# Merging the groups of full-f32 products in an indexer, a sparse attention and a stick-breaking attention

## The chip, the cores and the metric

The kernel runs on one core of a Trainium2 chip. The metric is the device time of one execution in microseconds. The engines of the core are named as in the profile: PE (TensorE matmuls), PEld (its weight loads), DVE (VectorE), ACT (ScalarE), POOL (GpSimd) and SP (SyncE, which here only issues transfers).

## The reference

Two layers (DEPTH = 2) on 256 tokens of width 2048. Each layer normalises its input, projects it once (`proj = h @ w_in`, 18064 columns) and feeds three token mixers; each mixer's output is gated, projected to 2048, and the three are merged with sigmoid gates before an output projection and the residual add. Cut to what the change touches:

```python
# A: sparse attention. 16 indexer heads score the keys, the best top_k = 64 of each query stay
rel   = einsum('bthd,bsd->bhts', qi, ki)
score = where(causal, einsum('bhts,bth->bts', relu(rel), wi), NEG_INF)
_, idx = top_k(score, 64)
p = softmax(where(valid, q @ ks * dh**-0.5, NEG_INF))     # 8 query heads, 2 key/value heads
o = p @ vs
# C: stick-breaking attention, 8 heads, strictly causal
z = q @ k * dh**-0.5
log_beta, log_keep = log_sigmoid(z), where(strict, log_sigmoid(-z), 0)
after = reverse_cumsum(log_keep) - log_keep
o = where(strict, exp(log_beta + after), 0) @ v
```

The queries and keys of A and of its indexer are rotated (rotary embedding) after the projection. All inputs and the output are float32.

## The kernel before, in words

**Units.** The work is a long row of projections. Each goes in units of 512 KB of weights: SP loads a unit (`raw`, four buffers), ACT rounds it to fp32r (`wh`, L223), DVE subtracts to get the rest (`wl`, L227); `wh` and `wl` have three buffers each. PE multiplies: in the usual unit (`chunk_N`) 8 products of 512 columns with `wh` and 4 with `wl`, all on L237. A chunk of 512 output columns over the 2048 inputs has 8 such units.

**Background steps.** What is not a projection is written as Python generators, the stages. After each unit, `background(mm)` first steps the pending transposes that are due and then advances at most one of the first two stages that are due; a stage's `yield n` means "not before n units from now". PE instructions of a step are put behind the last product of that unit (`issue_after`). Chunks that are wanted feature by feature (`chunk_F`) go through memory to be turned: DVE transposes 32x32 blocks (L265), POOL writes `z` to DRAM in four transfers (L268), two units later POOL reads it back as `zy` in one (L274), and after more units the consumer runs. For the query chunks QA the consumer is `rope_F`: two copies on ACT (L386, L387), and one unit later two products and a sum on DVE (L391, L392, L393), which write four heads of `qaT`. These consumer steps are issued with high priority behind the newest weight conversions (`behind`).

**Order.** An engine works in the order in which its instructions are written. That order is made when the kernel is built: a planner simulates the engines with its own costs, and at each moment gives a free engine the instruction of highest priority that its simulation holds to be ready. Conversions and transposes are marked high; all else goes by its place in the program. If on the chip an input comes later than the planner thought, the engine waits at that instruction.

**The steps that the change touches.** PSUM holds two `acc` tiles for projections and two `mm` tiles (1024 columns each) for everything else; `t4` has four buffers of 1024 columns; `ph`, `pl` one each.

- `index_first` scores tokens 64 to 127 with eight f32 products of 128 columns (L801) in two groups of four, `index` the second half with fp32r products (L830); then DVE selects the 64 best (`choose`, L788 to L791) and writes `bias`.
- `attend(t, c)`, one stage for each half of the queries t and each key/value head c, in the order (0,0), (1,0), (0,1), (1,1). It forms logits (L876 in f32 for t = 0, L873 in fp32r after a split for t = 1), softmax (L880 to L888, the exponentials on ACT at L885), turns the weights through memory, splits them into `ph` and `pl`, and multiplies with the values (L904). The four stages start after the chunk QC of the first four stick-breaking heads; in front of it come the two QA chunks.
- `stick(h0)`, one stage for two heads. It forms scores of two heads with f32 products (L942, L945), takes logarithms on ACT, splits, forms cumulative sums with fp32r products (L964 to L969), exponentials (L971), and the product with the values in f32 (L978, L980). Four stages, two of them in flight.

On the trace one f32 product is recorded as two matmuls.

Of the kernel before, what the change touches and what calls it, by code (L numbers as in the profile page):

```python
# [11 lines left out]
ALU = mybir.AluOpType  # L12
AX = mybir.AxisListType

P = 128
# [33 lines left out]
def trunk(ctx: ExitStack, tc: tile.TileContext, x, w_in, xt, w_a, w_b, w_c, w_out,  # L49
# [66 lines left out]
    def mm_tile():  # L116
        return mp.tile([P, 1024], F32, tag="mm", name=nm("mm"))
# [370 lines left out]
    for layer in range(DEPTH):  # L488
# [304 lines left out]
        def index_first(qi0=qi0, kiT=kiT, wi2=wi2, bias=bias):  # L793

            cb = cst[:, C_CB + P:C_CB + S]
            sc = tp.tile([P, S], F32, tag="sc", bufs=2, name=nm("sc"))[:, :P]
            bs = tp.tile([P, S], F32, tag="bias", bufs=2, name=nm("bias"))
            for g in range(2):
                ps = mm_tile()
                for q in range(4):  # L800
                    nc.tensor.matmul(ps[:, q * P:(q + 1) * P], qi0[:, (g * 4 + q) * P:(g * 4 + q + 1) * P], kiT[:, 0, :P],  # L801
                                     start=True, stop=True)
                rl = t4()[:, :512]
                nc.scalar.activation(rl, ps[:, :512], AF.Relu)
                for q in range(4):
                    i = g * 4 + q
                    if i == 0:
                        nc.vector.tensor_scalar(sc, rl[:, :P], wi2[:, :1], None, op0=ALU.mult)
                    else:
                        nc.vector.scalar_tensor_tensor(sc, rl[:, q * P:(q + 1) * P], wi2[:, i:i + 1], sc,  # L810
                                                       op0=ALU.mult, op1=ALU.add)
# [45 lines left out]
        finish()  # L857
        attended = []

        def attend(t, c, qaT=qaT, kaT=kaT, qk=qk, va=va, bias=bias, attended=attended):  # L860
            n = (t + 1) * P
            ts_ = slice(t * P, (t + 1) * P)
            if t:
                yield 4
                qp = [qk[:, 4 + i * 2:6 + i * 2, :].rearrange("p a (b t) -> p (a b) t", t=P) for i in range(2)]
                with behind():
                    split(*qp, qaT[:, c * 4:c * 4 + 4, ts_])
                yield 2
            ps = mm_tile()
            for q in range(4):  # L870
                if t:
                    for m, (i, j) in enumerate(((0, 0), (0, 1), (1, 0))):
                        nc.tensor.matmul(ps[:, q * n:(q + 1) * n], qp[i][:, q, :], qk[:, j * 2 + c, :],  # L873
                                         start=m == 0, stop=m == 2)
                else:
                    nc.tensor.matmul(ps[:, q * n:(q + 1) * n], qaT[:, c * 4 + q, ts_], kaT[:, c, :n],  # L876
                                     start=True, stop=True)
            lg = t4()
            l3 = lg[:, :4 * n].rearrange("p (h s) -> p h s", h=4)
            nc.vector.scalar_tensor_tensor(l3, ps[:, :4 * n].rearrange("p (h s) -> p h s", h=4), SCALE,  # L880
                                           heads(bias[t][:, :n], 4), op0=ALU.mult, op1=ALU.add)
            mx, sm = small(4), small(4)
            nc.vector.tensor_reduce(mx, l3, op=ALU.max, axis=AX.X, negate=True)  # L883
            for q in range(4):
# [3 lines left out]
            nc.vector.tensor_mul(l3, l3, sm.unsqueeze(2).to_broadcast([P, 4, n]))  # L888
            yield 4
            z = away([l3[:, :, s * P:(s + 1) * P] for s in range(t + 1)], t4()[:, :4 * n])  # L890
            yield 3
            y = lg[:, :4 * n].rearrange("p (u q i) -> p u q i", q=4, i=32)
            back(z, y)
            yield 7
            ph, pl = pair(1024)
            with behind():
                for s in range(t + 1):
                    split(*(v[:, s * 512:(s + 1) * 512].rearrange("p (q a i) -> p q a i", q=4, a=4) for v in (ph, pl)),
                          by_feature(y[:, s * 4:s * 4 + 4]))
            yield 3  # L900
            po = mm_tile()
            for s in range(t + 1):
                for i, (u, v) in enumerate(((va[0], ph), (va[0], pl), (va[1], ph))):
                    nc.tensor.matmul(po[:, :512], u[:, s, c * P:(c + 1) * P], v[:, s * 512:(s + 1) * 512],  # L904
                                     start=s == 0 and i == 0, stop=s == t and i == 2)
            nc.scalar.copy(qaT[:, c * 4:c * 4 + 4, ts_], po[:, :512].rearrange("p (h t) -> p h t", h=4))
            attended.append(c)

        for c in range(2):
            for t in range(NT):  # L910
                start(attend(t, c))
        chunk_F(w, O_QC + 4 * P, hx, KD, partial(use_q, 4))


# [22 lines left out]
                    b[:, 512:768].rearrange("p (h t) -> p h t", h=2))  # L937

        def stick(h0, qcT=qcT, kcT=kcT, vcr=vcr, diag=diag):
            ps = mm_tile()  # L940
            for q in range(2):
                nc.tensor.matmul(ps[:, q * S:(q + 1) * S], kcT[:, h0 + q, 0:P], qcT[:, h0 + q, :],  # L942
                                 start=True, stop=True)
            for q in range(2):
                nc.tensor.matmul(ps[:, 512 + q * P:512 + (q + 1) * P], kcT[:, h0 + q, P:S],  # L945
                                 qcT[:, h0 + q, P:S], start=True, stop=True)
            nk, lb = t4(), t4()
            ab = nc.scalar.activation(nk[:, :768], ps[:, :768], AF.Abs)
            with tc.issue_after(ab.ins):
                nc.scalar.preload_act_table_set("natural_log_exp_and_others")  # L950
            nc.scalar.activation(nk[:, :768], nk[:, :768], AF.Exp, scale=-1.0)
            nc.scalar.activation(nk[:, :768], nk[:, :768], AF.Ln, bias=1.0)
            nc.vector.scalar_tensor_tensor(lb[:, :768], ps[:, :768], 0.0, nk[:, :768],
                                           op0=ALU.min, op1=ALU.subtract)
            nc.vector.scalar_tensor_tensor(nk[:, :768], ps[:, :768], 0.0, nk[:, :768],
                                           op0=ALU.max, op1=ALU.add)
            for d in diag(nk):
                nc.vector.tensor_mul(d, d, smask2)
            pr_ = pair(768)
            split(*pr_, nk[:, :768])  # L960
            yield 8
            pc = mm_tile()
            for i, v in enumerate(pr_):
                nc.tensor.matmul(pc[:, :512], upper_r, v[:, :512], start=i == 0, stop=False)  # L964
            for i, v in enumerate(pr_):
                nc.tensor.matmul(pc[:, :512].rearrange("p (h t) -> p h t", h=2)[:, :, P:S], ones_r,  # L966
                                 v[:, 512:768].rearrange("p (h t) -> p h t", h=2), start=False, stop=i == 1)
            for i, v in enumerate(pr_):
                nc.tensor.matmul(pc[:, 512:768], upper_r, v[:, 512:768], start=i == 0, stop=i == 1)  # L969
            nc.vector.tensor_sub(lb[:, :768], lb[:, :768], pc[:, :768])  # L970
            nc.scalar.activation(lb[:, :768], lb[:, :768], AF.Exp)  # L971
            for d in diag(lb):
                nc.vector.tensor_mul(d, d, smask2)
            yield 5
            po = mm_tile()
            for q in range(2):
                vs_ = slice((h0 + q) * P, (h0 + q + 1) * P)
                nc.tensor.matmul(po[:, q * S:(q + 1) * S], vcr[:, 0, vs_], lb[:, q * S:(q + 1) * S],  # L978
                                 start=True, stop=False)
                nc.tensor.matmul(po[:, q * S + P:(q + 1) * S], vcr[:, 1, vs_],  # L980
                                 lb[:, 512 + q * P:512 + (q + 1) * P], start=False, stop=True)
# [236 lines left out]
```

## Time and profile before

| | |
|---|---|
| median of 3 runs | 2027.87 us (2027.77 to 2027.97) |
| profiled execution, its time | 2027.86 us |
| its span (first to last instruction) | 2026.0 us |
| PE busy | 2017.0 us, 100% of the span |
| DVE / ACT / POOL busy | 1515.5 / 1046.7 / 166.3 us |
| HBM read, written | 415.94 MB, 31.98 MB |
| granted TensorE clock | 0.999 |

The span and 1.86 us around it make up the execution's time. The busy shares are means over the whole program; what counts for a step is who waits for whom at its place. The profile's lines name the kernel line (L237), the tile written and the tiles read, and in brackets the idle time of the engine before the instruction and what ended it.

### The profile page before, as it was taken

What the parts mean: (1) busy time and instruction counts of PE and PEld (TensorE: products, weight loads), DVE (VectorE), ACT (ScalarE), POOL (GpSimd) and SP (SyncE); (2) the same over time, 40 slices, a digit from 0 to 9 for tenths busy, and PEclk for the clock granted to TensorE, in tenths of its full rate; (3) what the DMA queues carried; (4) which work ended last, traced back from release to release, by engine and by line L of the source; (5) the groups of instructions that cost most, each with busy time, mean ns of one, the idle gap of its engine ahead of it and who ended that gap; (6) DMA issues with size and microseconds to landing.
All of it is one profiled execution on the core that took longest, in us unless ns stands there. A gap on an engine that the chain in (4) does not pass through costs nothing.

```text
span 2026.0 us, 25968 instructions
## 1 busy us (share of the span) xinstructions
PE 2017.0 (100%) x9520; PEld 1694.7 (84%) x9520; DVE 1515.5 (75%) x2030; ACT 1046.7 (52%) x1213; POOL 166.3 (8%) x279
## 2 busy tenths in 40 slices
PE   9999999999999999999999999999999999999998
PEld 8889888888888888888888898888888888888887
DVE  8668998888788776555775789988886886756565
ACT  7456545566444454444554564555664444544543
POOL 0110022100010000010100101211000100101000
PEclk9999999999999999999999999999999999999999
DMA  7788678755576577776967876787555766677864
GB/s 260 232 292 240 184 245 280 246 178 166 175 236 195 183 221 234 218 234 213 306 203 232 285 222 200 249 263 246 176 166 177 233 196 193 212 252 214 251 222 151
DMA packets 235008, 449.64 MB, mean 222 GB/s; under 512 B 20992, under 2 KB 38400, under 8 KB 234752
## 3 DMA queue, kind: packets, MB, share of 16 engines
q1 hardware_dynamic: 215248, 389.25, 61.3%
q0 software_dynamic: 17968, 55.59, 8.9%
q10 hardware_dynamic: 1664, 3.15, 0.4%
q8 instruction: 74, 1.21, 0.3%
q14 instruction: 54, 0.44, 0.1%
HBM read 415.94 MB, written 31.98 MB: 221 GB/s over the span
## 4 chain that ended last, share of the span: by engine, by line
PE 100%; DVE 0%; ACT 0%; DVEq 0%; issue 0%
PE acc L237 93%; PE mm L237 3%; PE mm L830 1%; PE mm L904 0%; PE mm L978 0%; PE mm L942 0%; PE mm L873 0%; PE mm L618 0%; PE mm L964 0%; PE mm L876 0%; PE mm L801 0%; PE mm L945 0%; PE mm L980 0%; PE mm L969 0%; PE mm L966 0%; PE mm L995 0%
## 5 line engine op out<-in xcount | busy, mean ns | idle before, releaser
L237 PE MATMUL acc<-wh,s 128*128 128x512 f32 (+2 forms) x5632 | 1381.3, 387 | 0.0
L237 PEld LDWEIGHTS acc<-wh,s 128*128 128x128 f32 x5632 | 1038.8, 188 | 206.0 <-ACT wh L223 0.3
L227 DVE TENSOR_TENSOR wl<-raw,wh 128x1024 fp32r<-128x1024 f32 (+2 forms) x729 | 877.8, 1207 | 424.0 <-ACT wh L223 415.6
L223 ACT CAST wh<-raw 128x1024 fp32r<-128x1024 f32 (+2 forms) x728 | 758.3, 1043 | 837.0 <-PE acc L237 631.5
L237 PE MATMUL acc<-wl,s 128*128 128x512 f32 (+2 forms) x2624 | 691.0, 385 | 0.0
L237 PEld LDWEIGHTS acc<-wl,s 128*128 128x128 f32 x2624 | 487.7, 188 | 99.2
L268 POOL DMA_DIRECT2D z<-zt x184 | 106.9, 587 | 1454.0 <-DVE zt L265 1098.4
L440 DVE SCALAR_TENSOR_TENSOR s<-yT,cst,s 128x256 f32<-128x256 f32 x480 | 212.7, 479 | 0.0
L237 PEld LDWEIGHTS mm<-s,wl 128*128 128x128 f32 x512 | 66.9, 191 | 5.0
L237 PE MATMUL mm<-s,wl 128*128 128x192 f32 x512 | 66.0, 271 | 0.0
L274 POOL DMA_DIRECT2D zy<-z x47 | 33.8, 718 | 246.5 <-DMA z<-zt 127.9
L265 DVE STREAM_TRANSPOSE zt<-acc 128x512 f32<-128x512 f32 x64 | 44.6, 707 | 4.8 <-PE acc L237 4.7
L379 DVE TENSOR_TENSOR s<-zy,s 128x1024 fp32r<-128x1024 f32 x20 | 24.4, 1222 | 17.0 <-ACT s L378 17.0
L378 ACT CAST s<-zy 128x1024 fp32r<-128x1024 f32 x20 | 21.0, 1049 | 26.1 <-DMA zy<-z 18.4
L1070 DVE TENSOR_TENSOR ev<-acc,ev 128x512 f32<-128x512 f32 x32 | 22.0, 688 | 15.5 <-PE acc L237 15.5
L1060 ACT ACTIVATE ev<-acc 128x512 f32<-128x512 f32 x48 | 26.6, 592 | 0.1
L268 POOL DMA_DIRECT2D z<-t x36 | 20.4, 573 | 50.4 <-DVE t L265 49.3
L237 PE MATMUL acc<-s,wh 128*128 128x512 f32 x96 | 24.0, 392 | 0.0
L1071 DVE TENSOR_TENSOR s<-s,ev 128x512 f32<-128x512 f32 x32 | 21.9, 686 | 0.1
L1102 DVE TENSOR_TENSOR t<-acc,t 128x512 f32<-128x512 f32 (+1 forms) x18 | 10.6, 628 | 13.6 <-PE acc L237 13.6
L237 PEld LDWEIGHTS acc<-s,wh 128*128 128x128 f32 x96 | 17.3, 189 | 3.0
L885 ACT ACTIVATE t<-t,sm 128x128 f32<-128x128 f32 (+1 forms) x32 | 14.3, 448 | 9.4 <-DVE sm L883 9.4
(218 smaller groups left out, 867.5 us busy)
## 6 DMA issues: line engine op xcount, KB each, us to landing
raw<-in_w_in_dram SPq DMA_DIRECT2D x555, 512.0 KB, 4.4
raw<-in_w_out_dram SPq DMA_DIRECT2D x64, 512.0 KB, 4.9
zy<-z POOLq DMA_DIRECT2D x47, 512.0 KB, 5.4
z<-zt POOLq DMA_DIRECT2D x184, 128.0 KB, 4.3
raw<-in_w_a_dram SPq DMA_DIRECT2D x32, 512.0 KB, 4.1
raw<-in_w_c_dram SPq DMA_DIRECT2D x32, 512.0 KB, 3.6
raw<-in_w_b_dram SPq DMA_DIRECT2D x32, 512.0 KB, 4.9
raw<-in_w_in_dram SPq DMA_DIRECT2D x16, 256.0 KB, 3.0
```

What stands on the lines that cost most here:

```text
L223: newest_parts[0] = nc.scalar.copy(u[1], u[0])
L227: newest_parts[1] = sub = nc.vector.tensor_sub(u[2], u[0], u[1].bitcast(F32))
L237: newest[0] = nc.tensor.matmul(o, lhsT, rhs, start=start, stop=stop, skip_group_check=True)
L265: nc.vector.transpose(tmp[:, t].rearrange("p b k i -> p k b i"), src.rearrange("p k (b c) -> p k b c", b=4, c=32))
L268: nc.gpsimd.dma_start(z[:, :, :, a, :].rearrange("t b c e -> c (t b) e"), tmp[a * 32:(a + 1) * 32].rearrange("c t b k i -> c (t b) (k i)"))
L274: nc.gpsimd.dma_start(y.rearrange("p (t a) k i -> p t (a k i)", a=4), z.rearrange("t b c a e -> (b c) t (a e)"))
L378: nc.scalar.copy(h, src)
L379: nc.vector.tensor_sub(l, src, h.bitcast(F32))
L440: nc.vector.scalar_tensor_tensor(o, yT[:, c, q:q + S], wq, o, op0=ALU.mult, op1=ALU.add)
L1060: nc.scalar.activation(sg[t], g[t], AF.Sigmoid)
L1070: nc.vector.tensor_mul(sg[t], y[t], sg[t])
L1071: nc.vector.tensor_add(dst, dst, sg[t])
```

## The change

Three parts; the sums and products of the computation stay as they are.

1. `index_first` does its eight f32 products in one group, followed by one activation over 1024 columns, and yields once for 4 units instead of twice for 3.
2. `attend` takes a list of key/value heads. The first half of the queries (t = 0) is done for both heads in one stage: 8 products, one softmax of 1024 columns, one turn through memory, 6 value products in a row. The order of the stages becomes (t = 1, head 0), (t = 0, both heads), (t = 1, head 1). Since the second stage now reads all eight rotated heads, the QA consumer `use_a` notes which four heads it has written (`roped`), and a stage yields unit by unit until its heads are noted.
3. `stick` takes four heads: the scores of both pairs in both `mm` tiles at once, then the element-wise chain of each pair, the cumulative sums pair after pair with 3 units between, and one group of value products for four heads. One stage (`sticks`) runs the two groups of four one after the other; before, four stages of two heads ran two at a time.

The core of the diff:

```diff
-            for g in range(2):
-                ps = mm_tile()
-                for q in range(4):
-                    nc.tensor.matmul(ps[:, q * P:(q + 1) * P], qi0[...], kiT[:, 0, :P], start=True, stop=True)
-                rl = t4()[:, :512]
-                nc.scalar.activation(rl, ps[:, :512], AF.Relu)
...
-                yield 3
+            ps = mm_tile()
+            for i in range(NIH // 2):
+                nc.tensor.matmul(ps[:, i * P:(i + 1) * P], qi0[:, i * P:(i + 1) * P], kiT[:, 0, :P],
+                                 start=True, stop=True)
+            rl = t4()
+            nc.scalar.activation(rl, ps, AF.Relu)
...
+            yield 4
...
         qaT = slot()
+        roped = []
+
+        def use_a(h, y, qaT=qaT, roped=roped):
+            yield from rope_F(qaT[:, h:h + 4, :], y)
+            roped.append(h)
+
         for h in range(0, NH, 4):
-            chunk_F(w, O_QA + h * P, hx, KD, partial(rope_F, qaT[:, h:h + 4, :]), LATER - 1)
+            chunk_F(w, O_QA + h * P, hx, KD, partial(use_a, h), LATER - 1)
...
-        def attend(t, c, ...):
+        def attend(t, cs, ..., roped=roped, ...):
             n = (t + 1) * P
+            nh = 4 * len(cs)
+            blks = [(ci, s) for ci in range(len(cs)) for s in range(t + 1)]
+            while cs[-1] * 4 not in roped:
+                yield 1
             ts_ = slice(t * P, (t + 1) * P)
             if t:
                 yield 4
...
             ps = mm_tile()
-            for q in range(4):
+            for q in range(nh):
+                c = cs[q // 4]
...
-                    nc.tensor.matmul(ps[:, q * n:(q + 1) * n], qaT[:, c * 4 + q, ts_], kaT[:, c, :n],
+                    nc.tensor.matmul(ps[:, q * n:(q + 1) * n], qaT[:, c * 4 + q % 4, ts_], kaT[:, c, :n],
                                      start=True, stop=True)
...
-        for c in range(2):
-            for t in range(NT):
-                start(attend(t, c))
+        for job in ((1, (0,)), (0, (0, 1)), (1, (1,))):
+            start(attend(*job))
         chunk_F(w, O_QC + 4 * P, hx, KD, partial(use_q, 4))
...
         def stick(h0, ...):
-            ps = mm_tile()
-            for q in range(2):
...
+            pss = [mm_tile() for _ in range(2)]
+            for g, ps in enumerate(pss):
+                for q in range(2):
+                    h = h0 + g * 2 + q
...
+            pairs = []
+            for ps in pss:
+                nk, lb = t4(), t4()
...
+                pairs.append((nk, lb))
             pr_ = pair(768)
-            split(*pr_, nk[:, :768])
+            split(*pr_, pairs[0][0][:, :768])
             yield 8
...
+            for nk, lb in pairs:
+                if nk is not pairs[0][0]:
+                    pr_ = pair(768)
+                    split(*pr_, nk[:, :768])
+                    yield 3
+                pc = mm_tile()
...
-            yield 5
+            yield 4
             po = mm_tile()
-            for q in range(2):
+            for q in range(4):
...
-            nc.scalar.copy(qcT[:, h0:h0 + 2, :], po[:, :512].rearrange("p (h t) -> p h t", h=2))
+            nc.scalar.copy(qcT[:, h0:h0 + 4, :], po.rearrange("p (h t) -> p h t", h=4))
+            yield 2
...
-        for h0 in range(0, NH, 2):
-            start(stick(h0))
+        def sticks(stick=stick):
+            for h0 in range(0, NH, 4):
+                yield from stick(h0)
+
+        start(sticks())
```

More of the change, by code (lines that the diff above doesn't have):

```diff
@@ L797, in index_first @@
             bs = tp.tile([P, S], F32, tag="bias", bufs=2, name=nm("bias"))
-            for g in range(2):
-                ps = mm_tile()
-                for q in range(4):
-                    nc.tensor.matmul(ps[:, q * P:(q + 1) * P], qi0[:, (g * 4 + q) * P:(g * 4 + q + 1) * P], kiT[:, 0, :P],
-                                     start=True, stop=True)
-                rl = t4()[:, :512]
-                nc.scalar.activation(rl, ps[:, :512], AF.Relu)
-                for q in range(4):
[L806 to L811, printed above, removed]
-                yield 3
+            ps = mm_tile()
[4 more added lines that the diff above has]
+            nc.scalar.activation(rl, ps, AF.Relu)
+            for i in range(NIH // 2):
+                r_ = rl[:, i * P:(i + 1) * P]
+                if i == 0:
+                    nc.vector.tensor_scalar(sc, r_, wi2[:, :1], None, op0=ALU.mult)
+                else:
+                    nc.vector.scalar_tensor_tensor(sc, r_, wi2[:, i:i + 1], sc, op0=ALU.mult, op1=ALU.add)
+            yield 4
             up = slice(TOPK, P)
@@ L858, in trunk, with attend @@
         attended = []
-        def attend(t, c, qaT=qaT, kaT=kaT, qk=qk, va=va, bias=bias, attended=attended):
+        def attend(t, cs, qaT=qaT, roped=roped, kaT=kaT, qk=qk, va=va, bias=bias, attended=attended):
             n = (t + 1) * P
+            nh = 4 * len(cs)
+            blks = [(ci, s) for ci in range(len(cs)) for s in range(t + 1)]
+            while cs[-1] * 4 not in roped:
+                yield 1
             ts_ = slice(t * P, (t + 1) * P)
@@ L866, in attend @@
                 with behind():
-                    split(*qp, qaT[:, c * 4:c * 4 + 4, ts_])
+                    split(*qp, qaT[:, cs[0] * 4:cs[0] * 4 + 4, ts_])
                 yield 2
             ps = mm_tile()
-            for q in range(4):
+            for q in range(nh):
+                c = cs[q // 4]
                 if t:
@@ L875, in attend @@
                 else:
-                    nc.tensor.matmul(ps[:, q * n:(q + 1) * n], qaT[:, c * 4 + q, ts_], kaT[:, c, :n],
+                    nc.tensor.matmul(ps[:, q * n:(q + 1) * n], qaT[:, c * 4 + q % 4, ts_], kaT[:, c, :n],
                                      start=True, stop=True)
             lg = t4()
[L879 to L882, printed above, removed]
+            l3 = lg.rearrange("p (h s) -> p h s", h=nh)
+            nc.vector.scalar_tensor_tensor(l3, ps.rearrange("p (h s) -> p h s", h=nh), SCALE,
+                                           heads(bias[t][:, :n], nh), op0=ALU.mult, op1=ALU.add)
+            mx, sm = small(nh), small(nh)
             nc.vector.tensor_reduce(mx, l3, op=ALU.max, axis=AX.X, negate=True)
-            for q in range(4):
+            for q in range(nh):
                 nc.scalar.activation(l3[:, q, :], l3[:, q, :], AF.Exp, bias=mx[:, q:q + 1],
@@ L887, in attend @@
             nc.vector.reciprocal(sm, sm)
-            nc.vector.tensor_mul(l3, l3, sm.unsqueeze(2).to_broadcast([P, 4, n]))
+            nc.vector.tensor_mul(l3, l3, sm.unsqueeze(2).to_broadcast([P, nh, n]))
             yield 4
-            z = away([l3[:, :, s * P:(s + 1) * P] for s in range(t + 1)], t4()[:, :4 * n])
+            z = away([l3[:, ci * 4:ci * 4 + 4, s * P:(s + 1) * P] for ci, s in blks], t4())
             yield 3
-            y = lg[:, :4 * n].rearrange("p (u q i) -> p u q i", q=4, i=32)
+            y = lg.rearrange("p (u q i) -> p u q i", q=4, i=32)
             back(z, y)
@@ L939, in stick @@
         def stick(h0, qcT=qcT, kcT=kcT, vcr=vcr, diag=diag):
-            ps = mm_tile()
-            for q in range(2):
-                nc.tensor.matmul(ps[:, q * S:(q + 1) * S], kcT[:, h0 + q, 0:P], qcT[:, h0 + q, :],
-                                 start=True, stop=True)
-            for q in range(2):
-                nc.tensor.matmul(ps[:, 512 + q * P:512 + (q + 1) * P], kcT[:, h0 + q, P:S],
-                                 qcT[:, h0 + q, P:S], start=True, stop=True)
-            nk, lb = t4(), t4()
@@ L948, in stick @@
[L948 to L958, printed above, removed]
+            pss = [mm_tile() for _ in range(2)]
+            for g, ps in enumerate(pss):
+                for q in range(2):
+                    h = h0 + g * 2 + q
+                    nc.tensor.matmul(ps[:, q * S:(q + 1) * S], kcT[:, h, 0:P], qcT[:, h, :], start=True, stop=True)
+                for q in range(2):
+                    h = h0 + g * 2 + q
+                    nc.tensor.matmul(ps[:, 512 + q * P:512 + (q + 1) * P], kcT[:, h, P:S], qcT[:, h, P:S],
+                                     start=True, stop=True)
@@ new lines, in stick @@
+            pairs = []
+            for ps in pss:
+                nk, lb = t4(), t4()
+                ab = nc.scalar.activation(nk[:, :768], ps[:, :768], AF.Abs)
+                with tc.issue_after(ab.ins):
+                    nc.scalar.preload_act_table_set("natural_log_exp_and_others")
+                nc.scalar.activation(nk[:, :768], nk[:, :768], AF.Exp, scale=-1.0)
+                nc.scalar.activation(nk[:, :768], nk[:, :768], AF.Ln, bias=1.0)
+                nc.vector.scalar_tensor_tensor(lb[:, :768], ps[:, :768], 0.0, nk[:, :768],
+                                               op0=ALU.min, op1=ALU.subtract)
+                nc.vector.scalar_tensor_tensor(nk[:, :768], ps[:, :768], 0.0, nk[:, :768],
+                                               op0=ALU.max, op1=ALU.add)
+                for d in diag(nk):
+                    nc.vector.tensor_mul(d, d, smask2)
+                pairs.append((nk, lb))
@@ L959, in stick @@
             pr_ = pair(768)
-            split(*pr_, nk[:, :768])
+            split(*pr_, pairs[0][0][:, :768])
             yield 8
[L962 to L973, printed above, removed]
-            yield 5
+            for nk, lb in pairs:
[4 more added lines that the diff above has]
+                pc = mm_tile()
+                for i, v in enumerate(pr_):
+                    nc.tensor.matmul(pc[:, :512], upper_r, v[:, :512], start=i == 0, stop=False)
+                for i, v in enumerate(pr_):
+                    nc.tensor.matmul(pc[:, :512].rearrange("p (h t) -> p h t", h=2)[:, :, P:S], ones_r,
+                                     v[:, 512:768].rearrange("p (h t) -> p h t", h=2), start=False, stop=i == 1)
+                for i, v in enumerate(pr_):
+                    nc.tensor.matmul(pc[:, 512:768], upper_r, v[:, 512:768], start=i == 0, stop=i == 1)
+                nc.vector.tensor_sub(lb[:, :768], lb[:, :768], pc[:, :768])
+                nc.scalar.activation(lb[:, :768], lb[:, :768], AF.Exp)
+                for d in diag(lb):
+                    nc.vector.tensor_mul(d, d, smask2)
@@ L975, in stick @@
+            yield 4
             po = mm_tile()
-            for q in range(2):
+            for q in range(4):
+                lb, o = pairs[q // 2][1], q % 2
                 vs_ = slice((h0 + q) * P, (h0 + q + 1) * P)
-                nc.tensor.matmul(po[:, q * S:(q + 1) * S], vcr[:, 0, vs_], lb[:, q * S:(q + 1) * S],
+                nc.tensor.matmul(po[:, q * S:(q + 1) * S], vcr[:, 0, vs_], lb[:, o * S:(o + 1) * S],
                                  start=True, stop=False)
                 nc.tensor.matmul(po[:, q * S + P:(q + 1) * S], vcr[:, 1, vs_],
-                                 lb[:, 512 + q * P:512 + (q + 1) * P], start=False, stop=True)
@@ L982, in stick @@
-            nc.scalar.copy(qcT[:, h0:h0 + 2, :], po[:, :512].rearrange("p (h t) -> p h t", h=2))
-        for h0 in range(0, NH, 2):
-            start(stick(h0))
+                                 lb[:, 512 + o * P:512 + (o + 1) * P], start=False, stop=True)
+            nc.scalar.copy(qcT[:, h0:h0 + 4, :], po.rearrange("p (h t) -> p h t", h=4))
[4 more added lines that the diff above has]
+        start(sticks())
```

17 lines of the change are left out of this document (10 added, 7 removed).

## The prediction, made before the changed kernel was run

> **What bounds the kernel now.** I read the page first: busy times, then the chain that ended last.
>
> ```profile
> PE 2017.0 (100%) x9520; PEld 1694.7 (84%) x9520; DVE 1515.5 (75%) x2030; ACT 1046.7 (52%) x1213; POOL 166.3 (8%) x279
> PE 100%; DVE 0%; ACT 0%; DVEq 0%; issue 0%
> ```
>
> PE is busy through the span and is the whole chain. Whether busy PE also means that it never waits, the table of waits tells.
>
> ```profile
> PE mm L618 <- DVE eps L71: 1.1, 1, 1.1
> ACT wh L223 <- PE acc L237: 631.5, 447, 3.1
> ACT t L386 <- DMA zy<-z: 8.1, 2, 4.4
> ```
>
> Of PE there is one wait, at the start. The other engines run ahead of it: ACT waits 631.5 us for PE to free a `wh` buffer. So a change can help only by what it takes off PE itself, and harm only by making PE wait or by giving it more to do. The last row will matter: twice ACT stands before the rotation's copy for a transfer, up to 4.4 us.
>
> **What a group of f32 products costs PE.** The change keeps every product; it removes boundaries between groups. One stick-breaking group in the PE timeline:
>
> ```profile
> 432.01 1.07 PE L237 MATMUL acc<-wl,s 128*128 128x512 f32 x4
> 432.92 1.02 PE L942 MATMUL mm<-s,s 128*128 128x256 f32 x4
> 433.78 0.61 PE L945 MATMUL mm<-s,s 128*128 128x128 f32 x4
> 434.14 2.10 PE L237 MATMUL acc<-wh,s 128*128 128x512 f32 x8
> 436.08 1.08 PE L237 MATMUL acc<-wl,s 128*128 128x512 f32 x4
> ```
>
> And the place where sparse attention starts in layer 0:
>
> ```profile
> 268.85 1.98 PE L237 MATMUL acc<-wh,s 128*128 128x512 f32 x8
> 271.57 1.05 PE L876 MATMUL mm<-kaT,s 128*128 128x128 f32 x8
> 272.38 2.07 PE L237 MATMUL acc<-wh,s 128*128 128x512 f32 x8
> 275.20 1.98 PE L237 MATMUL acc<-wh,s 128*128 128x512 f32 x8
> 277.92 1.98 PE L237 MATMUL acc<-wh,s 128*128 128x512 f32 x8
> ```
>
> A unit takes 277.92 - 275.20 = 2.72 us from start to start. With a stick-breaking group in it, the distance from `wl` to `wl` is 436.08 - 432.01 = 4.07, so the group adds 1.35. Its own matmuls explain 433.78 - 432.92 = 0.86 for L942, and for four of L945 4 x 0.111 = 0.44 (the spacing from L876: 272.38 - 271.57 = 0.81 is seven spacings and the 0.03 by which the next record starts early). Left over: 0.05 us for one boundary. For L876: 275.20 - 268.85 - 2 x 2.72 = 0.91 against 8 x 0.111 = 0.89: 0.02. A mode change is nearly free here, and that is all the change can save on PE.
>
> **Part one, stick-breaking by fours.** In each layer four score groups become two and four value groups become two: 4 boundaries x 0.05 = 0.2 us, 0.4 in both layers. What is added is denser work on ACT and DVE and both `mm` and all four `t4` tiles held at once. I cost this at nothing: nobody else uses these tiles there (the gates' sigmoids that do are settled before), the yields leave 8, 3, 4 and 2 units, and the stage needs 2 x 17 = 34 units and one start, where 36 lie before the forced finish. The tightest old place was the second pair's split, one unit before its cumulative sums; the new distance is three units, 8.2 us. If the cover failed, PE would stop for one split; that is in the upper part of my range, not in the sum.
>
> **Part two, index_first in one group.** One boundary, 0.02 per layer. The selection on DVE starts two units earlier. DVE is busy nearly throughout there, so this moves what follows by a microsecond at most.
>
> **Part three, attention.** The f32 logits of t = 0 become one group (0.02 per layer), their value products too (fp32r, I take the stick group's 0.05). Four transfers and one read-back per layer go; POOL and the copies are off the path. All parts together: 2 x (0.20 + 0.02 + 0.02 + 0.05) = 0.6 us saved. Ends for this term: 0, and 1.7 us, if each of the 14 boundaries cost the full 2.10 - 1.98 = 0.12 by which the `wh` row after the group is longer.
>
> The reordering is what I price highest. Before, the first logits (L876 at 271.57) read the heads of the first QA chunk, rotated long ago. Now the stage for both heads is the second one. It is advanced after the second unit of the next chunk, in the very call that issues the last part of the rotation of heads 4 to 7. So eight of its sixteen records read what L393 writes in that moment. Will PE meet them too early? First, how late the rotation really is:
>
> ```profile
> 253.90 2.32 POOL L268 DMA_DIRECT2D z<-zt  x4 [19.30 <-DVE zt L265]
> 260.92 0.72 POOL L274 DMA_DIRECT2D zy<-z  x1 [4.70 <-DMA z<-zt]
> 262.71 1.06 ACT L223 CAST wh<-raw 128x1024 fp32r<-128x1024 f32 x1 [1.66 <-PE acc L237]
> 268.13 1.05 ACT L386 COPY t<-zy 64x1024 f32<-64x1024 f32 x1 [4.37 <-DMA zy<-z]
> 270.26 2.95 ACT L223 CAST wh<-raw 128x1024 fp32r<-128x1024 f32 x3
> 274.49 1.06 ACT L223 CAST wh<-raw 128x1024 fp32r<-128x1024 f32 x1 [1.28 <-PE acc L237]
> ```
>
> ACT finished a conversion at 263.77 and stood 4.37 us at the copy, with three conversions behind it that then ran back to back. The planner put the copy there because in its simulation the read-back had landed; on the chip it came over four microseconds later. DVE inherits this:
>
> ```profile
> 271.35 1.23 DVE L227 TENSOR_TENSOR wl<-raw,wh 128x1024 fp32r<-128x1024 f32 x1 [4.88 <-ACT wh L223]
> 272.49 1.22 DVE L391 TENSOR_TENSOR zy<-zy,cst 128x1024 f32<-128x1024 f32 x1
> 274.26 1.18 DVE L227 TENSOR_TENSOR wl<-raw,wh 128x1024 fp32r<-128x1024 f32 x1
> 275.36 1.22 DVE L392 TENSOR_TENSOR t<-t,cst 128x1024 f32<-128x1024 f32 x1
> 276.50 1.22 DVE L227 TENSOR_TENSOR wl<-raw,wh 128x1024 fp32r<-128x1024 f32 x1
> 278.26 1.18 DVE L393 TENSOR_TENSOR s<-zy,t 128x1024 f32<-128x1024 f32 x1
> 279.37 0.68 DVE L880 SCALAR_TENSOR_TENSOR t<-mm,bias 128x512 f32<-128x512 f32 x1
> 279.97 1.21 DVE L227 TENSOR_TENSOR wl<-raw,wh 128x1024 fp32r<-128x1024 f32 x1
> ```
>
> The rotation ends at 278.26 + 1.18 = 279.44. The three late conversions cost nothing before, since PE had up to three units in hand. Second, when did the planner think it would end? L880 has ordinary priority, yet it stands ahead of the conversion of 279.97, so that conversion was not ready in the simulation. Its `wh` was released by PE and cast at 274.49, ready at 275.55; so L393 had ended by about 275.5. The conversion in front of L393 (276.50) cannot have been ready before PE freed its buffer (eighth product of the unit at 268.85, about 270.7, plus a cast of 1.06): 271.7, then 1.13, a transpose of 0.63 and 1.18 give 274.7. So the planner has the rotation done between 274.7 and 275.5 on this clock.
>
> After the change the old L876 of 271.57 is gone, so the second unit ends 0.91 earlier, at 275.20 - 0.91 = 274.29. There the eight records of head group 0 are ready and run to 275.2. The eight of head group 1 follow at once or after at most two products of the next unit (0.45). On the chip their input exists at 279.44. PE stops for 279.44 - 275.20 = 4.24 us, or 3.8 if two products slip in. PE then has nothing else: its queue is in order. Layer 1 has the same picture:
>
> ```profile
> 1272.80 1.05 ACT L386 COPY t<-zy 64x1024 f32<-64x1024 f32 x1 [3.77 <-DMA zy<-z]
> 1280.47 1.98 PE L237 MATMUL acc<-wh,s 128*128 128x512 f32 x8
> 1283.19 1.98 PE L237 MATMUL acc<-wh,s 128*128 128x512 f32 x8
> 1282.93 1.19 DVE L393 TENSOR_TENSOR s<-zy,t 128x1024 f32<-128x1024 f32 x1
> 1284.03 0.69 DVE L880 SCALAR_TENSOR_TENSOR t<-mm,bias 128x512 f32<-128x512 f32 x1
> ```
>
> 1284.12 - 1280.47 = 3.65 us. Together 7.9 us, nothing hides them, and later waits are not recovered because PE has no slack to give. What is late next: nothing. The stop gives ACT and DVE back the lead that the late copy cost them, and the extra DVE work of the 1024-column softmax falls into that lead.
>
> **The sum.** 2027.86 (profiled execution, which equals the median to 0.01) + 7.9 - 0.6 = 2035.2 us. The rotation may end up to 1 us earlier or later in each layer because the index part is moved, and up to 0.9 us may slip in: 2032.3 to 2037.2 for this case alone.
>
> By the Trainium skill ("DMA: Bandwidth & Descriptors", section "Anatomy of one DMA — SWDGE (gpsimd) path") such a transfer takes about 2.0 us and its bytes over 436 GB/s, 3.2 us for the read-back's 512 KB: an estimate by which it lands ahead of ACT's turn and the sum is 2027.3. The trace disagrees: issued at 260.92, read at 268.13, 7.2 us, and the measurement decides.
>
> **The rivals.**
>
> No stop (not slower). The planner leaves the second half of the logits for two more units, to 275.20 + 2 x 2.72 = 280.6, after the real 279.44 and, in layer 1, 285.9 against 1284.12; or the read-back lands 4 us earlier because the index part is done sooner. It decides as soon as the rotation ends before PE's place. Then only the boundaries count: 2027.3 us. For it: no group on PE waited before, though many follow DVE. Against it: those did not follow a transfer by so few units, and the order of DVE bounds the planner's belief to 275.5.
>
> Half a stop. One more unit stands between: 279.44 - 277.92 = 1.52 and 1284.12 - 1283.19 = 0.93, so +2.45 - 0.6: 2029.7 us.
>
> A slow PE after the stop. At the start of the program PE is slow:
>
> ```profile
> 1.05 4.63 PE L618 MATMUL mm<-idle 128*128 128x128 f32 x20 [1.05 <-DVE eps L71]
> 5.34 2.87 PE L237 MATMUL acc<-wh,s 128*128 128x512 f32 x8
> ```
>
> Twenty records of 128 columns take 5.34 - 1.05 = 4.29, 0.215 each, against 0.111 later. If a stop of 4 us brings that pace back for some 6 us, about 3 us more are lost in each layer: 2041 us. For it: the stop is as long as 4.2 us. Against it: no row of this trace shows PE slow after a pause, since there is none. The Trainium skill ("TensorE: Matmul & The Clock Gate", section "What's actually happening") has half rate after an idle window of about 3.4 us and full rate after as long a busy one; the estimate by that is 1.7 us a layer where the free-running window lies within the stop, 2038.6 us. No run here shows it.
>
> The saving is larger than I think. Even 1.7 us is under the bound of 0.2% (4.06 us), which is about what a measurement of this kernel can tell from no change.
>
> **How the numbers follow.** The stop in both layers 0.57; no stop 0.23; half a stop 0.10; slow PE 0.07; a gain over 4 us, for which I have no mechanism, 0.03. Slower by over 0.2% (above 2031.9) is the first and the fourth: 0.64. Within 0.2% are no stop and half a stop: 0.33. Faster: 0.03. The range runs from just below the case without a stop, 2027.0, to 2037.5; outside are the slow PE, the gain and the upper tail of the first case, together about 0.15. The likeliest case alone has 2032.3 to 2037.2.
>
> **What would show it.** In the profile after, the waits of PE should have two new rows or one with two entries, PE at the f32 logits waiting for DVE at the rotation's sum, 3 to 4.5 us each, near 275 and 1284 us. ACT's wait at the rotation's copy should still be there. The distance from unit to unit in the stick-breaking stretch should stay 2.72, with groups of about 2.6 us. I am wrong if PE shows no wait there, if the logits of head group 1 stand units behind those of group 0, or if a wait appears in the stick-breaking part.

## The result, and the profile after

The changed kernel took 2039.16 us (median of 6 runs, 2036.24 to 2045.07) against 2027.89 us (2027.77 to 2028.00) before: ratio 1.0058, 95% interval 1.0048 to 1.0069. It is slower by 11.3 us, more than the 7.3 us predicted and outside the range that ended at 2037.5. The profiled execution took 2038.07 us, 10.2 more than the profiled one before; the account below is made for it.

The waits of PE, which had one row before (longest wait last in each row):

```profile
PE mm L886 <- DVE s L393: 5.3, 2, 3.2
PE mm L987 <- DVE pl L379: 2.1, 2, 1.1
PE mm L618 <- DVE eps L71: 1.1, 1, 1.1
PE acc L237 <- ACT wh L223: 0.7, 1, 0.7
```

The first row is the predicted one: the f32 logits (now L886) wait in both layers for the sum of the rotation. The second was not in the sum: the first product of a cumulative sum (L987) waits for a split. The PE timeline at the first place, layer 0:

```profile
271.45 1.98 PE L237 MATMUL acc<-wh,s 128*128 128x512 f32 x8
273.26 1.07 PE L237 MATMUL acc<-wl,s 128*128 128x512 f32 x4
274.17 1.05 PE L886 MATMUL mm<-kaT,s 128*128 128x128 f32 x8
278.42 2.08 PE L886 MATMUL mm<-kaT,s 128*128 128x128 f32 x8 [3.20 <-DVE s L393]
280.15 3.76 PE L237 MATMUL acc<-wh,s 128*128 128x512 f32 x8
283.71 1.39 PE L237 MATMUL acc<-wl,s 128*128 128x512 f32 x4
284.94 2.00 PE L237 MATMUL acc<-wh,s 128*128 128x512 f32 x8
```

The eight records of head group 0 run at 274.17, the next eight only at 278.42. From 274.17 to 278.42 are 4.25 us where eight records take 0.89: PE stands for 3.36 us. Then something else happens: the second eight take 1.73 us instead of 0.9, and the `wh` part of the next unit 283.71 - 280.15 = 3.56 instead of 1.81. The stretches of this kernel, cut into windows: the window, its length, the busy times of the engines beginning with PE, and at the end the granted clock, the DMA engines' busy share and GB/s:

```profile
274.90:278.30 3.40, 0.32 (x3) 0.13 (x2) 3.40 (x5) 0.13 (x1) 1.89 (x4) 0.89 0.47 130
278.30:284.50 6.20, 6.08 (x19) 5.17 (x20) 5.25 (x8) 0.55 (x1) 0.82 (x2) 0.51 0.83 269
284.50:300.00 15.50, 15.50 (x75) 13.06 (x74) 14.32 (x22) 10.74 (x24) 2.65 (x5) 1.00 0.69 189
```

PE is idle from 275.20 on; the clock falls 2.3 us later, still within the stop:

```profile
275.20:277.50 2.30, 0.02 (x1) 0.00 (x0) 2.30 (x4) 0.00 (x0) 1.08 (x2) 1.00 0.36 63
277.50:278.40 0.90, 0.00 (x0) 0.00 (x0) 0.90 (x2) 0.00 (x0) 0.90 (x3) 0.52 0.98 369
```

By the trace's clock records it stood at half from 277.54 to 284.37, 6.83 us. In layer 1, by the PE timeline and then by windows, the stop is shorter and the clock stays whole:

```profile
1286.60 1.05 PE L886 MATMUL mm<-kaT,s 128*128 128x128 f32 x8
1289.71 1.16 PE L886 MATMUL mm<-kaT,s 128*128 128x128 f32 x8 [2.07 <-DVE s L393]
1290.63 2.09 PE L237 MATMUL acc<-wh,s 128*128 128x512 f32 x8
```

The windows of the same place:

```profile
1286.60:1289.70 3.10, 1.05 (x9) 0.85 (x7) 3.10 (x5) 0.85 (x2) 1.99 (x4) 1.00 0.57 157
1289.70:1296.00 6.30, 6.29 (x32) 5.36 (x33) 6.30 (x9) 3.21 (x5) 0.85 (x2) 1.00 0.83 256
```

Here it is 1289.71 - 1286.60 - 0.89 = 2.2 us. What PE waited for, on ACT and on DVE in layer 0:

```profile
267.05 1.05 ACT L386 COPY t<-zy 64x1024 f32<-64x1024 f32 x1 [3.21 <-DMA zy<-z]
271.41 1.22 DVE L391 TENSOR_TENSOR zy<-zy,cst 128x1024 f32<-128x1024 f32 x1
277.15 1.21 DVE L393 TENSOR_TENSOR s<-zy,t 128x1024 f32<-128x1024 f32 x1
```

ACT stood 3.21 us for the read-back, and the rotation ended at 278.36, where PE goes on.

The second place, in the second four heads of stick-breaking, on all three engines:

```profile
499.49 1.28 ACT L967 ACT_TABLE_LOAD   x1
501.86 1.28 ACT L1088 ACT_TABLE_LOAD   x1
505.20 1.28 ACT L968 ACT_TABLE_LOAD   x1
508.30 1.28 ACT L969 ACT_TABLE_LOAD   x1
509.59 0.85 ACT L969 ACTIVATE t<-t 128x768 f32<-128x768 f32 x1
511.28 0.83 ACT L378 CAST ph<-t 128x768 fp32r<-128x768 f32 x1
516.87 0.40 PE L987 MATMUL mm<-ph,upper_r 128*128 128x512 f32 x1
516.88 0.76 DVE L975 TENSOR_TENSOR t<-t,cst 128x256 f32<-128x256 f32 x2
517.55 0.95 DVE L379 TENSOR_TENSOR pl<-t,ph 128x768 fp32r<-128x768 f32 x1
518.56 0.50 PE L987 MATMUL mm<-pl,upper_r 128*128 128x512 f32 x1 [1.06 <-DVE pl L379]
```

The second pair's chain (L967 to L969 on ACT, L970 to L975 on DVE) meets the sigmoid of a merge gate (L1088), which takes the table away; the exponential and the logarithm load theirs again. The split of the first pair (L378, L379) stands behind that chain on both engines although its input is long ready, so `pl` exists at 518.50, and PE, at 516.87, has to stop. In the first four heads of layer 0 no gate falls into the chain, and PE does not wait.

How far the projections of the changed kernel lie behind those of the kernel before, at the same unit (start in the one less start in the other): -0.12 us before the attention of layer 0, +6.08 after it, +7.04 after stick-breaking, +7.03 before and +9.33 after the attention of layer 1, +10.27 after its stick-breaking and at the end. All of it arises in these four stretches, and none is given back.

### The profile page after: what moved, and what is told of

Read it like the earlier page. It is cut to its first block, busy times and chain, and to the rows that moved or that the text cites. A ratio compares the mean times of both kernels' runs of the same rounds, so it can differ in the third digit from the quotient of the medians.

```text
span 2036.3 us, 25934 instructions
## 1 busy us (share of the span) xinstructions
PE 2019.2 (99%) x9520; PEld 1696.0 (83%) x9520; DVE 1516.2 (74%) x2022; ACT 1047.9 (51%) x1211; POOL 161.3 (8%) x269
## 4 chain that ended last, share of the span: by engine, by line
PE 98%; DVE 1%; DMA 0%; ACT 0%; SPq 0%; issue 0%; DVEq 0%
PE acc L237 93%; PE mm L237 3%; PE mm L828 1%; PE mm L915 0%; PE mm L1002 0%; PE mm L957 0%; PE mm L883 0%; DMA raw<-in_w_in_dram 0%; DVE wl L227 0%; PE mm L987 0%; PE mm L800 0%; PE mm L960 0%; PE mm L1004 0%; PE mm L886 0%; DVE s L393 0%; PE mm L992 0%
## 5 line engine op out<-in xcount | busy, mean ns | idle before, releaser
L379 DVE TENSOR_TENSOR s<-zy,s 128x1024 fp32r<-128x1024 f32 x20 | 24.4, 1222 | 24.7 <-ACT s L378 24.7
L378 ACT CAST s<-zy 128x1024 fp32r<-128x1024 f32 x20 | 21.0, 1049 | 34.3 <-DMA zy<-z 26.2
L1088 ACT ACTIVATE ev<-acc 128x512 f32<-128x512 f32 x48 | 26.5, 591 | 0.1
L268 POOL DMA_DIRECT2D z<-t x28 | 16.3, 587 | 51.9 <-DVE t L265 51.9
L970 DVE SCALAR_TENSOR_TENSOR t<-mm,t 128x768 f32<-128x768 f32 x8 | 7.6, 956 | 15.4 <-ACT t L969 15.4
```

The costliest lines, as they stand in the source:

```text
L268: nc.gpsimd.dma_start(z[:, :, :, a, :].rearrange("t b c e -> c (t b) e"), tmp[a * 32:(a + 1) * 32].rearrange("c t b k i -> c (t b) (k i)"))
L378: nc.scalar.copy(h, src)
L379: nc.vector.tensor_sub(l, src, h.bitcast(F32))
L1088: nc.scalar.activation(sg[t], g[t], AF.Sigmoid)
```

## The experiments

Each kernel was run against the kernel before on the same chip; the kernel before had a median of 2027.82 us in the first four and 2027.88 us in the last three.

**E1: logits of both heads two units later.**

```diff
             while cs[-1] * 4 not in roped:
                 yield 1
+            if not t:
+                yield 2
```

> The logits of both heads are issued two units later than in the change, everything else as in the change. Theory (the planner believes the rotation done about 3 us before the chip has it done, because of the late read-back; PE stops at the second half of these logits, and after a stop of about 3.4 us runs at half pace for some 6 us): no wait of PE at the logits in either layer, granted clock 1.0 throughout, little spread between runs. Left are the two waits of 1.2 us in front of the cumulative sums of the second four heads, less the boundaries saved: 2028.8 to 2029.5 us. Rival (the merged softmax and turn through memory overload ACT and DVE, and the lost time comes from there): time stays above 2035 us, waits of PE on weight conversions appear.

Measured: 2030.50 us (2029.86 to 2036.02, 11 runs), ratio 1.0018 (1.0009 to 1.0027). In the profiled execution (2030.33 us) the wait at the logits is gone and the other one is unchanged:

```profile
PE mm L989 <- DVE pl L379: 2.1, 2, 1.1
PE mm L618 <- DVE eps L71: 1.1, 1, 1.1
PE acc L237 <- DVE wl L227: 0.4, 1, 0.4
```

So the merged softmax does not cost by its size; the distance between the rotation and the logits does. The median lies 1 us over the expectation, and two runs lie over 2034: ACT still waits for the read-back (7.9 us over four copies), and the last row shows that now conversions come late too. The run of 2036.02 us has a mean clock of 0.998 where the others have 0.999, so a slow stretch may lie in it; no profile of it was taken.

**E2: the first pair's split ahead of the second pair's chain.**

```diff
                 pairs.append((nk, lb))
-            pr_ = pair(768)
-            split(*pr_, pairs[0][0][:, :768])
+                if len(pairs) == 1:
+                    pr_ = pair(768)
+                    split(*pr_, nk[:, :768])
             yield 8
```

> The split of the first pair's logarithms stands ahead of the second pair's element-wise chain; the rest as in the change. Theory (the first pair's split sits behind the second pair's chain, which two more table loads delay): the two waits of PE in front of the cumulative sums, 1.06 us each plus the pace lost around them, 2.5 us together, go; the stop at the logits stays, 2 to 4 us a layer, and so does the spread: median about 2036.5 us. Rival (the two score groups at once simply fill ACT, so the order of the split does not matter): the waits stay at about 1 us and the time at the change's 2039.

Measured: 2037.83 us (2034.91 to 2039.20, 5 runs), ratio 1.0046 (1.0034 to 1.0059); the median lies 1.3 us over the expectation. The waits in front of the cumulative sums are gone, the stop at the logits is there, longer in layer 0 this time (1.4 us in layer 1). ACT stood 5.3 us for the read-back of layer 0, and one of the two waits in the second row is there too: a conversion came 0.88 us late. PE's waits:

```profile
PE mm L886 <- DVE s L393: 5.6, 2, 4.2
PE acc L237 <- ACT wh L223: 1.8, 2, 0.9
```

The stop, the records behind it and what follows, in windows, with the clock third from the end; the last row takes the second and the third together:

```profile
276.70:280.80 4.10, 0.00 (x0) 0.00 (x0) 4.10 (x6) 0.00 (x0) 1.98 (x4) 1.00 0.48 145
280.80:281.70 0.90, 0.88 (x7) 0.88 (x8) 0.90 (x1) 0.00 (x0) 0.34 (x1) 1.00 1.16 271
281.70:285.20 3.50, 3.50 (x11) 2.82 (x10) 3.50 (x7) 0.00 (x0) 0.00 (x0) 0.51 0.95 311
280.80:285.20 4.40, 4.38 (x16) 3.70 (x17) 4.40 (x7) 0.00 (x0) 0.34 (x1) 0.61 0.99 303
```

The clock fell to half after that stop again, here only 0.9 us after PE had gone on, and for a shorter time: 3.41 us by the clock records (mean 0.61 over 4.4 us). That the order of the split makes the second wait is shown.

**E3: both edits.**

> Both edits together: logits of both heads two units later, first pair's split ahead of the second pair's chain. Theory: no wait of PE after the first microseconds, clock 1.0, and only the boundaries saved count: 14 groups fewer, 0.6 to 0.9 us, so 2027.0 to 2027.3 us, slightly under the kernel before. Rival (fuller groups cost PE something of their own, for example slower weight loads in long f32 groups): 2028 us or more with no waits to show for it.

Measured: 2027.42 us (2026.55 to 2030.19, 11 runs), ratio 0.9999 (0.9991 to 1.0008). The profiled execution took 2026.79 us, 1.07 less than the one before the change, with one wait of PE beside that of the start, 0.5 us in the first microseconds. By the distance at equal units stick-breaking alone is now 0.34 us shorter in each layer, attention 0.07 and 0.00; 0.18 is the start. So the boundaries are worth about 0.8 us, and fuller groups cost PE nothing in this execution. The median is 0.4 us under the kernel before, though the interval takes in 1; three runs at 2029 to 2030 remain, and no profile of them was taken.

**E4: the stop filled with work.**

```diff
             for q in range(nh):
                 c = cs[q // 4]
+                if q == 4:
+                    fill = mm_tile()
+                    for _ in range(10):
+                        nc.tensor.matmul(fill[:, :P], kaT[:, 0, :P], kaT[:, 0, :P], start=True, stop=True)
```

> As the change, with ten extra f32 products of 128 columns (results unused) on PE between the logits of head group 0 and those of head group 1, 2.2 us of work placed where PE stands still. Theory (half pace follows because PE was idle for about 3.4 us): the place costs as much as before, since the rotation ends when it ends, but the idle part falls to about 1 us, so the granted clock stays 1.0 in every run; about 2.9 us less than the change where it ran slow once, 2035 us, and runs within 1.5 us of each other. Rival (the slow stretch comes from the long f32 groups or from chance, not from idleness): clock still 0.5 for some 6 us after layer 0's stop, median 2039 or more, spread as wide as the change's 9 us.

Measured: 2035.99 us (2035.34 to 2037.54, 5 runs), ratio 1.0041 (1.0027 to 1.0054), 1 us over the expectation. In layer 1 the fill covers the stop whole. The PE timeline at the place in layer 0:

```profile
274.31 1.05 PE L890 MATMUL mm<-kaT,s 128*128 128x128 f32 x8
275.20 2.40 PE L884 MATMUL mm<-kaT 128*128 128x128 f32 x20
279.28 1.16 PE L890 MATMUL mm<-kaT,s 128*128 128x128 f32 x8 [1.69 <-DVE s L393]
280.20 2.10 PE L237 MATMUL acc<-wh,s 128*128 128x512 f32 x8
282.14 1.08 PE L237 MATMUL acc<-wl,s 128*128 128x512 f32 x4
```

The window that begins with the second eight records:

```profile
279.30:285.50 6.20, 6.20 (x31) 5.29 (x32) 6.20 (x11) 2.33 (x2) 0.76 (x2) 1.00 0.81 260
```

The rotation ends even later here (PE goes on at 279.28 against 278.42), yet the clock stays at 1.00, with the DMA engines as busy as in the change (0.81 against 0.83): the second eight records take 0.92 and the `wh` part 1.94 us. All five runs have a mean clock of 0.999, and they spread over 2.2 us, where the changed kernel has 0.996 to 0.998 and spreads over 8.8 us. With more work on PE the median is 3.2 us lower than that of the change, though the two intervals overlap. The slow stretch comes from idleness, not from the f32 groups.

**E5: the rotation two units later, the logits still right behind it.** E2's edit, and:

```diff
-            chunk_F(w, O_QA + h * P, hx, KD, partial(use_a, h), LATER - 1)
+            chunk_F(w, O_QA + h * P, hx, KD, partial(use_a, h), LATER + 1 if h else LATER - 1)
```

> The change with the split of the first pair moved ahead (as before), and with the rotation of heads 4 to 7 two units later; the logits of both heads are still issued in the very call that issues the last part of that rotation. Theory (PE stopped because the read-back lands some 4 us after the planner thinks; with two units more it has landed when ACT comes to the copy, and planner and chip agree): ACT does not wait at the rotation's copy, PE does not wait at the logits, conversions keep their lead, and no run is a few us over the others: 2026.8 to 2027.2 us with a spread under 1 us. Rival (logits issued right behind the rotation that they read must wait for it on the chip, whatever the transfer does): PE waits 2 to 4 us at the logits as in the change, 2032 us or more.

Measured: 2026.90 us (2026.68 to 2027.93, 11 runs) against 2027.88 us (2027.53 to 2029.27, 27 runs), ratio 0.9996 (0.9987 to 1.0004). ACT comes to the copy after a late conversion and finds the read-back landed; PE goes through the logits in one piece of sixteen records:

```profile
269.25 1.05 ACT L386 COPY t<-zy 64x1024 f32<-64x1024 f32 x1
277.62 1.22 DVE L393 TENSOR_TENSOR s<-zy,t 128x1024 f32<-128x1024 f32 x1
279.63 1.95 PE L886 MATMUL mm<-kaT,s 128*128 128x128 f32 x16
281.33 2.07 PE L237 MATMUL acc<-wh,s 128*128 128x512 f32 x8
```

The rotation ends at 278.84, 0.8 us before PE asks for it. Being issued right behind the rotation does no harm as long as the planner's picture of the transfer holds. The spread is 1.3 us, a little over the 1 us expected. The slow tail of E1 and E3 is gone together with ACT's wait; that the wait made the tail was not tried by itself. This version has the lowest median, 1.0 us under the kernel before, though the interval of the ratio takes in 1.

**E6: the stick-breaking part alone on the kernel before.**

> The kernel before with the stick-breaking part of the change alone. Theory (the parts add up: per layer 1.31 us of stop at the first pair's split of the second four heads, less 0.35 us for four boundaries): 0.96 us a layer, 2029.7 to 2029.9 us, two waits of PE of 1.1 us, and no more spread than before. Rival (the stops in front of the cumulative sums are an echo of the late attention, shifted stages meeting each other): no wait there, 2027.2 us.

Measured: 2029.71 us (2029.33 to 2031.53, 10 runs), ratio 1.0009 (1.0000 to 1.0019). Two waits of 1.1 us at the cumulative sum, as in the change:

```profile
PE mm L975 <- DVE pl L379: 2.1, 2, 1.1
```

At equal units stick-breaking costs 0.98 and 0.96 us here, as in the change: this part does not depend on the attention. The profiled execution, 2030.58 us, is 2.72 us longer than the one before: the other 0.8 us are 0.2 at the start and 0.6 in the attention of layer 1, which this kernel did not change. There ACT stood 5.25 us for the read-back, and about 19 us later PE waited 0.29 us for a conversion; that the one made the other is not shown.

**E7: the kernel before with the later rotation.** E5's change of `LATER`, here on `rope_F`.

> The kernel before with the rotation of heads 4 to 7 two units later. Theory (ACT's wait of 4.4 us at the copy was covered by the units that PE had in hand, so it costs nothing before the change and taking it away gains nothing): the wait at the copy gone or under 1 us, time within 0.3 us of before. Rival (the late conversions behind that copy did slow PE a little, or the later rotation collides with the next transfers): over 0.5 us away from before.

Measured: 2027.86 us (2027.59 to 2028.27, 11 runs), ratio 0.9999 (0.9990 to 1.0008). ACT waits at none of the four copies, and nothing is gained: the 4.4 us that ACT stood there before the change were covered in full. They were covered only just: where ACT stood 4.54 us (E1) and 5.32 us (E2) in layer 0, PE waited 0.42 and 0.88 us for a conversion soon after.

## Why the prediction was right and where it was wrong

**The stop at the logits: right in mechanism and place, too long.** The planner put the second eight records where the working said, directly behind the first (PE asks at 275.06 in layer 0), and E1 and E5 show the cause. The term was 7.9 us; the profiled execution has 3.36 + 2.2 = 5.6. What was mis-sized is the end of the rotation: 278.36 instead of 279.44 in layer 0, since the read-back landed 1.1 us sooner (ACT's wait of 3.21 instead of 4.37); in layer 1 that wait was 2.29 instead of 3.77. In E2, whose attention is the same, ACT stood 5.32 and 1.60 us and PE 4.2 and 1.4, so one profiled execution does not fix this landing. A small slip of the working leaves the forecast as it was: at 3.2 us from 260.92 the read-back would have landed at 264.12, 0.35 us behind ACT's turn at 263.77 and not ahead of it.

**"What is late next: nothing" was wrong, twice.** First, the slow PE. It was a rival with a chance of 0.07, held down because no row showed PE after a pause. It happened. From 278.42 on the three pieces before the clock is whole again take 1.73, 3.56 and 1.23 us where E4's rows and the ordinary unit have 0.92, 1.94 and 0.91: 2.8 us lost, close to the 3 us that I priced for a layer; in E2 it was 1.6 us. The stops of 3.36 us and of 4.3 us (E2) brought it, 2.2 us and E4's 1.7 us did not. The rule of the Trainium skill ("TensorE: Matmul & The Clock Gate", section "What's actually happening") is half rate after an idle window of about 3.4 us that runs freely. These traces agree with the free-running window: every stretch of one clock that lies within the runs is a whole multiple of 3.41 us (6.83 at half in the change and 3.41 in E2, and 1747.62 at full rate, 512 times as long, between the change's slow stretch and its end). They do not agree that it must be idle throughout: the window that ended with the fall at 277.54 began at 274.13 with 1.1 us of work, and the one of E2, which ended at 281.75, closed with 0.9 us of work. About 2.3 and 2.5 us of idleness in a window were enough. In layer 1 the steps, counted on from 284.37, put 1.8 us of the stop into one window, and that was not enough. I had the rule, a stop forecast at 4.24 us, and gave it far too little weight. That the prediction's 2038.6 us lies near the measured time is luck: it has the full 7.9 us, a slow stretch in both layers and nothing for the split.

**Second, the stick-breaking part: the cover failed.** I costed the denser work at nothing because the yields leave 8 units, and put a stop only into the upper part of the range. The wait appeared in both layers, and a wait there was the prediction's own last sign of being wrong. The step that failed is "the tightest old place was the second pair's split": the tight one is the first pair's, which the change moves behind the second pair's whole chain. E2 and E3 show it, E6 that it stands by itself. Without the wait the part gains 0.34 us a layer (E3), with it it loses 0.95, so a stop with its loss is 1.3 us, 2.6 for both layers. That further table loads make the chain late is read from the rows (four of 1.28 us between 499.49 and 509.58); it was not tried by itself.

**The boundaries: right.** 0.6 us was the estimate, about 0.8 is what E3 and E5 show, nearly all of it in stick-breaking (0.34 a layer where the sum had 0.20), and the upper end of 1.7 held. None of the forms that were tried gained 0.2%.

The account of the profiled execution: 5.6 + 2.8 + 2.6 - 0.8 - 0.1 (start) = 10.1 us against 10.2 measured. The median of the runs is 1 us above it; longer runs have a lower mean clock (0.998 at 2036.24 us, 0.996 at 2045.07), so they probably hold more of the slow stretches; how much, and in which layer, is not seen without a profile of each.

## What to carry to other kernels

Where one engine is the whole chain, ask of every reordering which instruction on it now follows a transfer or an in-order chain closely, and compare the place in its queue with when the input really exists: a wait of another engine that costs nothing may become a stop of this one. When a stop of TensorE of about 3 us or more is forecast (here 3.36 us brought half rate and 2.2 us did not), the half-rate stretch behind it belongs into the sum, not among the rivals. And when two element-wise chains are put into one step, issue what the bounding engine reads first ahead of the second chain.

## What the runs showed of the hardware beyond expectation

- Filling a stop with useless matmuls kept the granted clock at 1.00 where the same place ran at half for 6.83 us, and the runs spread over 2.2 us instead of 8.8.
- The granted clock changed only at steps of 3.41 us: half rate lasted two steps (6.83 us) after a stop of 3.36 us, and one step (3.41 us) after a stop of 4.3 us in E2, so the longer stop cost less behind it (1.6 against 2.8 us). In E2 PE stood 4.1 us at a clock of 1.00, and the clock fell only after PE had gone on.
- A TensorE boundary between f32 and fp32r groups costs less than a tenth of a microsecond. E5's sixteen records in one group add 4.51 - 2.72 = 1.79 us to the unit, two groups of eight 2 x 0.91 = 1.82; in stick-breaking four boundaries are worth 0.34 us a layer.
